# Twelve loads of a streaming encoder layer, issued by GpSimd instead of SyncE

## The chip, the cores and the metric

The kernel runs on one core of a Trainium2 chip. The metric is the device time of one execution in microseconds, the median of several runs. The five engines are named as the profile names them: PE (TensorE), DVE (VectorE), ACT (ScalarE), POOL (GpSimd) and SP (SyncE, which here only issues transfers). Each engine works through its own list of instructions in order; a transfer is issued by an instruction of an engine and then runs on the DMA engines by itself.

## What is computed

One layer of a streaming encoder for 384 rows: 256 prompt frames of one new stream and 16 frames of each of 8 running streams, all in float32.

```python
h = rmsnorm(x)                      # 384 x 2048
p = h @ w_in                        # columns: GLU in (2 x 1024) | q | k | v | forget logits | gates A, B
u = p[glu value] * sigmoid(p[glu gate])
A = conv branch: 31-tap causal depthwise conv over (old conv state, u), LayerNorm, swish, @ conv_pw_out
B = attention with a forget bias: running streams see 128 cached keys and values each; @ w_att_out
x = x + (sigmoid(gA) * A + sigmoid(gB) * B) @ w_out
x = x + (silu(conv3(g_half)) * u_half) @ w_down     # g_half, u_half = rmsnorm(x) @ w_up, d_ff 5632
```

Outputs are both groups' rows, the new keys, values and forget logits, and the new conv states.

## The kernel before

**Products.** Every large product streams its weights from HBM in tiles of 256 x 512 (`raw`, three buffers, issued by SP, `fetch`, L130). Each tile is split into `hi`, a rounded copy made by ACT (L139), and `lo`, the rest, made by DVE (L140); both have two buffers. PE then does three matmuls per block, hi by hi, lo by hi and hi by lo (L236 to L238), so PE needs each tile's `lo` soon after its `hi`. `gemm` walks through the tiles; after each 128 rows of weights it calls `tick`, which takes one step of each side job (generators). One such step of 9 matmuls is 2 us of PE at 512 columns.

**Side jobs in the first stages.** The stages are GLU (two pairs of a gate and a value product, 64 steps), V (48 steps), K and Q (32 each), then the gates. Beside them run:

- `weight_columns`: loads the old conv states, transposes them in 32 x 32 blocks on DVE (L250) and writes them through POOL to a DRAM tile `s_rows` (`quadrants_out`, four stores, L255). A load back from such a tile completes the transposition.
- `glu_pair`: when a pair is finished, `u` is evacuated, transposed the same way and written to `u_rows` by four POOL stores.
- `conv`: `load(n)` brings half of the old states (`sc`) and of the turned gated input (`uc`) back from `s_rows` and `u_rows`; `fill(c)` copies them on ACT into a tile `ext` (two buffers, L480 to L489; two small memsets by POOL, L482 and L483); `tap` does 31 multiply-adds on DVE (L496, L498) for each of eight tiles. The first `load` is emitted at step 37, the first `fill` at step 45, the second `load` with the 23rd tap of the third tile.
- `cached_keys`: from step 40 on, one head every 14 steps: the load `kc` of 128 keys of 8 streams (512 KB in rows of 512 bytes, L567), nine steps later the DVE transpose into `kw` (L250), then four POOL stores to a DRAM tile `keys`. `kc` and `kw` have one buffer each. The attention stage reads `keys` back by SP.

**What sets the order.** PE's order is the program's. For the other engines a planner in the tile framework lists the instructions ahead of time, by a priority that follows the order of the program (weight tiles and evacuations are raised by `high_priority`) and by its own idea of when each operand is ready; it may put an instruction far ahead of its place in the program. The list is then fixed, and the engine stops at an instruction whose operand is not there. `queued` adds one rule: a transfer is listed behind the newest transfer noted for its engine; with `False` as second argument it only becomes the newest. The transfers of later weight tiles are noted so, without being held. In the kernel before, all `queued` transfers but two go out on SP, and the stores of `quadrants_out` are not noted.

Of the kernel before, what the change touches and what calls it, by code (L numbers as in the profile page):

```python
# [40 lines left out]
def hybrid_step(  # L41
# [9 lines left out]
    nc = tc.nc  # L51
# [39 lines left out]
    def queued(d, chain=True):  # L91
        e = d.ins.engine
        if chain and e in newest:
            tc.add_manual_dep(d.ins, newest[e], mybir.DependencyInfo(
                mybir.DependencyClass.NoSync, mybir.DependencyReason.DATA), reason="queue")
        newest[e] = d.ins.name
# [152 lines left out]
    def swap_blocks(dst, src, q):  # L249
        nc.vector.transpose(dst.rearrange("p i q c -> p q i c"), src.rearrange("p (q i c) -> p q i c", q=q, i=4))  # L250

    def quadrants_out(src, n, d=None):
        d = d or p_dr.tile([4, 32, 4, n], F32, tag="turn", bufs=4, name="turn")
        for i in range(4):
            nc.gpsimd.dma_start(d[:, :, i, :].rearrange("j r n -> r j n"),  # L255
                                src[32 * i:32 * i + 32, :].rearrange("r (j n) -> r j n", j=4))
        return d

    def quadrants_in(dst, d, queue=None):
# [2 lines left out]
    def turned(rows, work, out):  # L262
        w = work.rearrange("p (i t q c) -> p i t q c", i=4, t=NTT, c=32)
        for t in range(NTT):
            swap_blocks(w[:, :, t], rows[:, t, :], 4)
        quadrants_in(out, quadrants_out(work, 384))
        return out.rearrange("p (i t q c) -> p i t q c", i=4, t=NTT, q=4)
# [173 lines left out]
    u_rows = [p_dr.tile([4, 32, 4, 384], F32, name=f"u_rows{i}") for i in range(2)]  # L441
    s_rows = p_dr.tile([4, 32, 4, 2, 256], F32, name="s_rows")

    def glu_pair(i):
        u = p_sg.tile([P, NTT, 512], F32, tag=f"S{2 + i}", name="u")
        cs = slice(512 * i, 512 * (i + 1))

        def gate(t, ps):
            nc.scalar.activation(u[:, t, :], ps[:], AF.Sigmoid, scale=rs1[:, t:t + 1])

        def value(t, ps):
            stt(u[:, t, :], ps[:], rs1[:, t:t + 1], u[:, t, :], op0=ALU.mult, op1=ALU.mult)

        def done():
            for t in range(NTT):
                swap_blocks(u_work[:, :, t], u[:, t, :], 4)
            quadrants_out(u_work[:].rearrange("p i t q c -> p (i t q c)"), 384, u_rows[i])
            nc.gpsimd.dma_start(sample_conv[0, :, 14:30, cs], u[:, 2, :])
            nc.gpsimd.dma_start(prompt_conv[0, 0, :, cs], u[98:128, 1, :])
        return job("B", 16, ha, gate), job("B", 16, ha, value, done=done)  # L460
# [3 lines left out]
    def conv():  # L464
        states, news, exts = {}, {}, {}

        def load(n):
            states[n] = p_cv.tile([P, 8, 4, 32], F32, tag="sc", bufs=1, name="sc")
            queued(nc.sync.dma_start(states[n][:].rearrange("p b q c -> p b (q c)"),
                                     s_rows[:, :, :, :, 128 * n:128 * (n + 1)].rearrange("j r i h n -> (j r) (i h) n")))  # L470
            news[n] = p_cv.tile([P, 4, NTT, 4, 32], F32, tag="uc", bufs=1, name="uc")
            queued(nc.sync.dma_start(news[n][:].rearrange("p i t q c -> p (i t q c)"),
                                     u_rows[n][:].rearrange("j r i n -> (j r) (i n)")))

        def fill(c):
            ext = exts[c] = p_cv.tile([P, 24, 46], F32, tag="ext", bufs=2, name="ext")
            e = ext[:].rearrange("p (i t h) x -> p i t h x", t=NTT, h=2)
            u = news[c // 4][:, :, :, c % 4, :].rearrange("p i t (h x) -> p i t h x", h=2)
            copy = nc.scalar.copy
            copy(e[:, :, 2, :, 0:30], states[c // 4][:, :, c % 4, 0:30].rearrange("p (i h) x -> p i h x", h=2))  # L480
            copy(ext[:, :, 30:46].rearrange("p (a h) x -> p a h x", h=2), u.rearrange("p i t h x -> p (i t) h x"))
            nc.gpsimd.memset(ext[:, 0, 0:30], 0.0)  # L482
            nc.gpsimd.memset(ext[:, 1, 0:14], 0.0)  # L483
            copy(e[:, :, 0:2, 1, 14:30], u[:, :, 0:2, 0, :])
            copy(e[:, 1:4, 0:2, 0, 14:30], u[:, 0:3, 0:2, 1, :])
            copy(e[:, 0, 1, 0, 14:30], u[:, 3, 0, 1, :])
            for h in range(2):
                copy(e[:, 1:4, 0:2, h, 0:14], u[:, 0:3, 0:2, h, 2:16])
            copy(e[:, 0, 1, :, 0:14], u[:, 3, 0, :, 2:16])  # L489

        def tap(c, w):
            v = exts[c][:, :, w:w + 16]
            o = ut[:, c, :].rearrange("p (a t) -> p a t", t=16)
            wc = cw[:, w * 8 + c:w * 8 + c + 1]
            if w == 0:
                ts(o, v, wc, col[:, R_DWB + c:R_DWB + c + 1], op0=ALU.mult, op1=ALU.add)  # L496
            else:
                stt(o, v, wc, o, op0=ALU.mult, op1=ALU.add)  # L498
            if w == CW - 1:
                if c == 1:  # L500
                    nc.gpsimd.tensor_tensor(sm[:], ut[:, 0, :], ut[:, 1, :], op=ALU.add)
                elif c > 1:
                    nc.gpsimd.tensor_tensor(sm[:], sm[:], ut[:, c, :], op=ALU.add)

        todo = [(c, w) for c in range(8) for w in range(CW)]
        done = due = 0
        for t in range(1 << 20):
            due += next(r for end, r in CONV_RATE if t < end)
            if t == CONV_START - 9:
                load(0)  # L510
            if t == CONV_START - 1:
                fill(0)
            while done < min(due, len(todo)):
                c, w = todo[done]
                tap(c, w)
                if w == 22 and c < 7:
                    fill(c + 1)
                    if c == 2:
                        load(1)
                done += 1  # L520
            if done == len(todo):
                return
            yield
# [38 lines left out]
    def cached_keys():  # L562
        for _ in range(KEYS_FIRST):
            yield
        for h in range(H):
            kc, work = (p_sg.tile([P, 8, P], F32, tag=f"S{i}", name=n) for i, n in enumerate(("kc", "kw")))
            queued(nc.sync.dma_start(kc[:], cache_k[0, :, :, h, :].rearrange("b p d -> p b d")))  # L567
            for _ in range(9):
                yield
            swap_blocks(work[:].rearrange("p b d -> p (b d)").rearrange("p (i b c) -> p i b c", i=4, b=8),  # L570
                        kc[:].rearrange("p b d -> p (b d)"), 8)
            key_rows[h] = p_dr.tile([4, 32, 4, 256], F32, name=f"keys{h}")
            quadrants_out(work[:].rearrange("p b d -> p (b d)"), 256, key_rows[h])
            for _ in range(KEYS_EVERY - 9):
                yield

    key_steps = cached_keys()

    gemm([glu_pair(i) for i in range(2)], [first_norm(), weight_columns(), conv_steps, key_steps])
# [4 lines left out]
    def tiny(name):  # L584
        return p_qkv.tile([P, NTT, H], F32, name=name)

    z, e, r, s2, pl = tiny("lz"), tiny("le"), tiny("lr"), tiny("ls"), tiny("lpoly")
# [531 lines left out]
```

## Time and profile before

| | us |
|---|---|
| median of 3 runs (lowest, highest) | 1997.26 (1996.68, 1998.42) |
| profiled execution | 1996.12 |
| its span, first to last instruction | 1994.4 |
| PE busy | 1982.1 |
| DVE, ACT, POOL busy | 1050.5, 774.4, 229.1 |

SP's transfer queue (q1) moved 275.16 MB, POOL's (q0) 67.69 MB. Times within the trace count from the start of the span. A timeline lists an engine's instructions by their start, with their duration; a bracket says how long the engine stood idle before one and which instruction or transfer ended that. The granted clock is TensorE's, as a share of full speed.

### The profile page before, as it was taken

To read this page: it belongs to the slowest core of one execution; us is meant where nothing else is said; L and a number is where in the kernel's file an instruction comes from. 1 tells how busy PE (TensorE), PEld (TensorE's weight loads), DVE (VectorE), ACT (ScalarE), POOL (GpSimd) and SP (SyncE) were. 2 spreads that over 40 slices of the span, in tenths; PEclk is the share of its full clock that TensorE was granted. 3 is DMA by queue.
4 is the path that set the end of the run, shared out by engine and by line. 5 is a ranking of instruction groups with operands and counts; after the bars stand their busy time and mean duration, and the time that the engine had idled before them with its cause. 6 is when DMAs were issued, how large, how long until landed. Compare 5 with 4: busy or idle time off the path is not lost.

```text
span 1994.4 us, 24094 instructions
## 1 busy us (share of the span) xinstructions
PE 1982.1 (99%) x9156; PEld 1645.2 (82%) x9156; DVE 1050.5 (53%) x1479; ACT 774.4 (39%) x1149; POOL 229.1 (11%) x492
## 2 busy tenths in 40 slices
PE   9999999999999999999999999999999999999999
PEld 7779888888888888888888888888888888888887
DVE  4489989643335447445454555343554554334543
ACT  4433353654324433445343444222433442223422
POOL 2002231100000002011211112000211120002100
PEclk9999999999999999999999999999999999999999
DMA  8556876654443448565656565444555554446553
GB/s 238 160 163 196 269 235 194 206 179 134 127 127 118 136 153 276 179 192 173 215 160 195 165 189 172 150 132 129 175 175 183 176 184 133 130 132 193 159 187 119
DMA packets 182563, 344.52 MB, mean 173 GB/s; under 512 B 15160, under 2 KB 47811, under 8 KB 182439
## 3 DMA queue, kind: packets, MB, share of 16 engines
q1 hardware_dynamic: 163711, 275.16, 45.1%
q0 software_dynamic: 18416, 67.69, 10.7%
q8 instruction: 71, 1.16, 0.2%
q14 instruction: 45, 0.37, 0.1%
q10 hardware_dynamic: 320, 0.14, 0.0%
HBM read 301.26 MB, written 42.14 MB: 172 GB/s over the span
## 4 chain that ended last, share of the span: by engine, by line
PE 90%; DVE 6%; issue 1%; DMA 1%; ACT 1%; POOL 0%; SPq 0%; DVEq 0%; POOLq 0%; ACTq 0%
PE acc L237 29%; PE acc L236 29%; PE acc L238 29%; DVE ut L498 3%; DVE lo L140 2%; PE misc L236 1%; PE misc L238 1%; PE misc L237 1%; DMA kc<-in_cache_k_dram 1%; DMA uc<-u_rows 0%; DVE qkw L250 0%; ACT hi L139 0%; PE misc L300 0%; PE misc L719 0%; PE misc L752 0%
## 5 line engine op out<-in xcount | busy, mean ns | idle before, releaser
L140 DVE TENSOR_TENSOR lo<-raw,hi 128x1024 fp32r<-128x1024 f32 (+2 forms) x481 | 579.5, 1205 | 828.3 <-ACT hi L139 822.3
L139 ACT CAST hi<-raw 128x1024 fp32r<-128x1024 f32 (+2 forms) x481 | 499.7, 1039 | 1062.0 <-PE acc L238 952.2
L237 PE MATMUL acc<-lo,xg 128*128 128x512 f32 x1056 | 410.9, 389 | 0.1
L238 PE MATMUL acc<-hi,xg 128*128 128x512 f32 x1056 | 410.8, 389 | 0.0
L236 PE MATMUL acc<-hi,xg 128*128 128x512 f32 x1056 | 410.8, 389 | 0.0
L237 PE MATMUL acc<-lo,hT 128*128 128x512 f32 (+1 forms) x880 | 334.1, 380 | 4.2 <-DVE lo L140 4.1
L236 PE MATMUL acc<-hi,hT 128*128 128x512 f32 (+1 forms) x880 | 337.9, 384 | 0.3 <-ACT hi L139 0.3
L238 PE MATMUL acc<-hi,hT 128*128 128x512 f32 (+1 forms) x880 | 333.8, 379 | 0.0
L237 PEld LDWEIGHTS acc<-lo,xg 128*128 128x128 f32 x1056 | 198.2, 188 | 41.6 <-DVE lo L140 0.5
L236 PEld LDWEIGHTS acc<-hi,xg 128*128 128x128 f32 x1056 | 198.2, 188 | 41.3
L238 PEld LDWEIGHTS acc<-hi,xg 128*128 128x128 f32 x1056 | 198.2, 188 | 41.1
L237 PEld LDWEIGHTS acc<-lo,hT 128*128 128x128 f32 x880 | 165.7, 188 | 36.3 <-DVE lo L140 8.9
L236 PEld LDWEIGHTS acc<-hi,hT 128*128 128x128 f32 x880 | 165.5, 188 | 30.4 <-issue 1.8
L238 PEld LDWEIGHTS acc<-hi,hT 128*128 128x128 f32 x880 | 165.4, 188 | 28.9
L236 PE MATMUL acc<-hi,act 128*128 128x512 f32 x484 | 188.3, 389 | 0.0
L237 PE MATMUL acc<-lo,act 128*128 128x512 f32 x484 | 188.3, 389 | 0.0
L238 PE MATMUL acc<-hi,act 128*128 128x512 f32 x484 | 188.3, 389 | 0.0
L255 POOL DMA_DIRECT2D turn<-block x124 | 68.1, 556 | 1031.5 <-DVE block L250 1004.9
L498 DVE SCALAR_TENSOR_TENSOR ut<-ext,cw,ut 128x384 f32<-128x384 f32 x240 | 138.4, 628 | 1.0
L238 PEld LDWEIGHTS acc<-hi,act 128*128 128x128 f32 x484 | 90.8, 188 | 19.0
L237 PEld LDWEIGHTS acc<-lo,act 128*128 128x128 f32 x484 | 90.8, 188 | 18.8
L236 PEld LDWEIGHTS acc<-hi,act 128*128 128x128 f32 x484 | 90.8, 188 | 18.7
(286 smaller groups left out, 1761.9 us busy)
## 6 DMA issues: line engine op xcount, KB each, us to landing
raw<-in_w_up_dram SPq DMA_DIRECT2D x176, 512.0 KB
raw<-in_w_in_dram SPq DMA_DIRECT2D x127, 512.0 KB
raw<-in_w_down_dram SPq DMA_DIRECT2D x88, 512.0 KB
turn<-block POOLq DMA_DIRECT2D x120, 192.0 KB, 4.1
block<-turn POOLq DMA_DIRECT2D x30, 768.0 KB, 6.0
raw<-in_w_out_dram SPq DMA_DIRECT2D x32, 512.0 KB
raw<-in_w_in_dram SPq DMA_DIRECT2D x24, 344.0 KB
raw<-in_w_att_out_dram SPq DMA_DIRECT2D x16, 512.0 KB
```

The source lines that it names most:

```text
L139: nc.scalar.copy(hi[:, k, :o], raw[:, k, :o])
L140: tt(lo[:, k, :o], raw[:, k, :o], f(hi[:, k, :o]), op=ALU.subtract)
L236: mm(o, ah[:, s], hi[:, kk, :n], start=st, stop=False)
L237: mm(o, ah[:, s], lo[:, kk, :n], start=False, stop=False)
L238: mm(o, al[:, s], hi[:, kk, :n], start=False, stop=sp)
L255: nc.gpsimd.dma_start(d[:, :, i, :].rearrange("j r n -> r j n"), src[32 * i:32 * i + 32, :].rearrange("r (j n) -> r j n", j=4))
L498: stt(o, v, wc, o, op0=ALU.mult, op1=ALU.add)
```

## The change

The eight loads of `kc`, the two of `sc` and the two of `uc` are issued by POOL instead of SP. The four stores of `quadrants_out`, on POOL before and after, are now noted as POOL's newest transfer, so that each of these loads is listed behind the POOL store or load emitted last before it. Nothing else is altered; the loads of `keys` by SP stay.

```diff
     def quadrants_out(src, n, d=None):
         d = d or p_dr.tile([4, 32, 4, n], F32, tag="turn", bufs=4, name="turn")
         for i in range(4):
-            nc.gpsimd.dma_start(d[:, :, i, :].rearrange("j r n -> r j n"),
-                                src[32 * i:32 * i + 32, :].rearrange("r (j n) -> r j n", j=4))
+            queued(nc.gpsimd.dma_start(d[:, :, i, :].rearrange("j r n -> r j n"),
+                                       src[32 * i:32 * i + 32, :].rearrange("r (j n) -> r j n", j=4)), False)
         return d
...
             states[n] = p_cv.tile([P, 8, 4, 32], F32, tag="sc", bufs=1, name="sc")
-            queued(nc.sync.dma_start(states[n][:].rearrange("p b q c -> p b (q c)"),
+            queued(nc.gpsimd.dma_start(states[n][:].rearrange("p b q c -> p b (q c)"),
...
             news[n] = p_cv.tile([P, 4, NTT, 4, 32], F32, tag="uc", bufs=1, name="uc")
-            queued(nc.sync.dma_start(news[n][:].rearrange("p i t q c -> p (i t q c)"),
+            queued(nc.gpsimd.dma_start(news[n][:].rearrange("p i t q c -> p (i t q c)"),
...
-            queued(nc.sync.dma_start(kc[:], cache_k[0, :, :, h, :].rearrange("b p d -> p b d")))
+            queued(nc.gpsimd.dma_start(kc[:], cache_k[0, :, :, h, :].rearrange("b p d -> p b d")))
```

## Rows read from the trace of the kernel before

**Rows 1.** The page, part 1: busy us, share of the span, instructions of each engine.

```profile
PE 1982.1 (99%) x9156; PEld 1645.2 (82%) x9156; DVE 1050.5 (53%) x1479; ACT 774.4 (39%) x1149; POOL 229.1 (11%) x492
```

**Rows 2.** Stretches, PE alone: from and to, us, busy, granted clock, DMA share, GB/s.

```profile
0.00:25.00 25.00, 21.81 (x108) 1.00 0.82 247
...
1975.00:2000.00 25.00, 14.86 (x66) 0.91 0.09 32
```

**Rows 3.** Timeline of PE: matmuls that waited, 80 to 140; start, us, instruction.

```profile
81.45 0.50 PE L237 MATMUL acc<-lo,hT 128*128 128x512 f32 x1 [0.25 <-DVE lo L140]
99.28 0.50 PE L237 MATMUL acc<-lo,hT 128*128 128x512 f32 x1 [1.23 <-DVE lo L140]
113.65 0.50 PE L237 MATMUL acc<-lo,hT 128*128 128x512 f32 x1 [1.69 <-DVE lo L140]
```

**Rows 4.** Stretches of 2 us: PE, PEld, DVE, ACT, POOL busy, granted clock, DMA.

```profile
112.00:114.00 2.00, 0.35 (x2) 0.31 (x3) 2.00 (x3) 0.72 (x1) 0.00 (x0) 1.00 0.00 0
114.00:116.00 2.00, 2.00 (x8) 1.57 (x7) 2.00 (x5) 0.00 (x0) 0.00 (x0) 0.67 0.60 146
116.00:118.00 2.00, 2.00 (x6) 1.58 (x5) 2.00 (x4) 0.00 (x0) 0.00 (x0) 0.50 0.30 116
118.00:120.00 2.00, 2.00 (x10) 1.59 (x9) 2.00 (x5) 0.55 (x1) 0.00 (x0) 0.97 0.76 197
```

**Rows 5.** Timeline of DVE, 90 to 113.

```profile
90.80 1.22 DVE L140 TENSOR_TENSOR lo<-raw,hi 128x1024 fp32r<-128x1024 f32 x1 [2.85 <-ACT hi L139]
96.88 1.25 DVE L250 STREAM_TRANSPOSE kw<-kc 128x1024 f32<-128x1024 f32 x1 [4.85 <-DMA kc<-in_cache_k_dram]
...
109.22 0.48 DVE L496 TENSOR_SCALAR ut<-ext,cw,col 128x384 f32<-128x384 f32 x1 [3.39 <-ACT ext L489]
...
112.37 1.22 DVE L140 TENSOR_TENSOR lo<-raw,hi 128x1024 fp32r<-128x1024 f32 x1
```

**Rows 6.** The chain that ended last: start, us from issue to landing.

```profile
88.38 8.47 DMA kc<-in_cache_k_dram
...
99.79 7.85 DMA uc<-u_rows
```

**Rows 7.** Timeline of ACT, 107 to 111.

```profile
107.67 0.52 ACT L481 COPY ext<-uc 128x384 f32<-128x384 f32 x1 [3.10 <-DMA uc<-u_rows]
...
110.36 1.05 ACT L139 CAST hi<-raw 128x1024 fp32r<-128x1024 f32 x1
```

**Rows 8.** Timeline of SP: its issues (xcount: that many within the time).

```profile
88.38 1.48 SPq L567 DMA_DIRECT2D kc<-in_cache_k_dram  x1
92.05 7.57 SPq L130 DMA_DIRECT2D raw<-in_w_in_dram  x2
...
268.17 0.46 SPq L567 DMA_DIRECT2D kc<-in_cache_k_dram  x1
```

**Rows 9.** Timeline of POOL, first stages and feed-forward part.

```profile
10.89 0.12 POOL L482 MEMSET ext<- 128x30 f32 x1
...
86.61 2.18 POOL L255 DMA_DIRECT2D u_rows<-u_work  x4 [1.16 <-DVE u_work L250]
98.42 2.18 POOL L255 DMA_DIRECT2D keys<-kw  x4 [9.62 <-DVE kw L250]
...
983.33 2.19 POOL L255 DMA_DIRECT2D turn<-block  x4 [5.19 <-DVE block L250]
991.54 0.56 POOL L260 DMA_DIRECT2D block<-turn  x1 [6.02 <-DMA turn<-block]
```

**Rows 10.** Line 260, POOL's loads of turned tiles.

```profile
DMA to landing us min/median/max: 4.5/5.8/7.2
```

**Rows 11.** Waits: engine, line, waited for; us in total, times, longest us.

```profile
DVE kw L250 <- DMA kc<-in_cache_k_dram: 6.7, 3, 4.9
...
ACT block L953 <- DMA block<-turn: 2.0, 4, 0.6
...
ACT extf L1000 <- DMA block<-turn: 0.8, 1, 0.8
```

More of the change, by code (lines that the diff above doesn't have):

```diff
@@ L468, in load @@
             states[n] = p_cv.tile([P, 8, 4, 32], F32, tag="sc", bufs=1, name="sc")
-            queued(nc.sync.dma_start(states[n][:].rearrange("p b q c -> p b (q c)"),
-                                     s_rows[:, :, :, :, 128 * n:128 * (n + 1)].rearrange("j r i h n -> (j r) (i h) n")))
+            queued(nc.gpsimd.dma_start(states[n][:].rearrange("p b q c -> p b (q c)"),
+                                       s_rows[:, :, :, :, 128 * n:128 * (n + 1)].rearrange("j r i h n -> (j r) (i h) n")))
             news[n] = p_cv.tile([P, 4, NTT, 4, 32], F32, tag="uc", bufs=1, name="uc")
-            queued(nc.sync.dma_start(news[n][:].rearrange("p i t q c -> p (i t q c)"),
-                                     u_rows[n][:].rearrange("j r i n -> (j r) (i n)")))
+            queued(nc.gpsimd.dma_start(news[n][:].rearrange("p i t q c -> p (i t q c)"),
+                                       u_rows[n][:].rearrange("j r i n -> (j r) (i n)")))
         def fill(c):
```

## The prediction

> **What bounds the kernel now.** I read the page's busy table first, then PE's busy time in stretches of 25 us, then every place where a matmul waited, and only there the other engines. The reader is to see that TensorE is the bound nearly everywhere: it is busy for 1982.1 us [rows 1] of a span of 1994.4, so only 12.3 us are idle in all. Of these, the first 25 us hold 25.00 - 21.81 = 3.19 and the tail after 1975 holds 19.4 - 14.86 = 4.54 [rows 2], and neither is near the change. The other 4.57 us lie in between, most of them in two places, both in the second half of the GLU stage: 1.23 us ahead of the matmul at 99.28 and 1.69 us ahead of the one at 113.65 [rows 3]. Both end when VectorE delivers a split weight (lo). A third wait, 0.25 us at 81.45, comes from VectorE's own evacuation work there, and I leave it as it is.
>
> The second wait has a consequence that idle time does not show. Right behind it the granted clock is 0.67, 0.50 and 0.97 in three stretches of 2 us [rows 4], before and after it 1.00: the engine runs partly at 1.2 instead of 2.4 GHz, and loses 2 x (0.33 + 0.50 + 0.03) = 1.72 us. The shorter wait at 98 has no such fall behind it. So what can be won here is 1.23 + 1.69 + 1.72 = 4.64 us, 0.23% of the time; even if every idle moment between start and tail went too, it would be 4.57 + 1.72 = 6.3 us.
>
> **Why these two waits are there.** At 96.88 VectorE turns the first cached-key tile (kw from kc). It works in order, so it stood still for 4.85 us until kc had landed [rows 5]; SP had issued kc at 88.38, 8.47 us earlier [rows 6]. The lo behind it came late, and PE waited 1.23 us. Then ScalarE waited 3.10 us for uc, the turned gated input, which was issued at 99.79 and took 7.85 us [rows 6]. The twelve copies of two conv tiles ran from 107.67 to 110.36, where the next weight's hi starts [rows 7]; VectorE first waited 3.39 us for them and then worked on conv taps from 109.22 to 112.37, ahead of the lo that PE needed [rows 5]. Both loads landed later than the order on an in-order engine had room for.
>
> **The change part by part.**
>
> *SP gives up twelve issues* (eight kc, two sc, two uc). One occupies SP for 0.46 to 1.48 us [rows 8]. But SP is not short of time: the lo at 90.80 ends at 92.02 [rows 5], and the weight that waits for its buffer is issued at 92.05 [rows 8]. Gain: 0. The cover is the three weight buffers; without it, one long issue of 1.48 us would stand in a weight's way.
>
> *POOL takes twelve issues.* The four stores of a turned block take 2.18 us [rows 9], so one issue is 0.55 and twelve are 6.5 us, on an engine that is busy 11% of the span [rows 1]. Price on the path: 0. The bytes stay the same, 8 x 0.52 + 2 x 0.52 + 2 x 0.79 = 6.8 MB, which leave SP's queue for POOL's.
>
> *The new order.* Each store now counts as the newest transfer of POOL, and each load is put behind the newest. In program order these are the stores of u_rows, then sc, uc, then kc of head 0, so on POOL this order is forced: the u_rows stores are issued from 86.61 to 88.79 [rows 9], sc right behind, and uc must wait until the stores have landed. How long that is, the same pair shows later: stores issued until 985.52, the load at 991.54, 6.0 us behind [rows 9]. uc is then issued at 94.8 and kc at 95.4. Meanwhile POOL holds up nothing that is wanted: its next work now is at 98.42 [rows 9], and that itself follows from kc. A load of this pattern lands in 4.5 to 7.2 us [rows 10]; the two that SP issued here took 7.85 and 8.47. So uc lands at 99.3 to 102.6 instead of 107.64, and kc at 99.9 to 103.9 instead of 96.85: uc 5 to 8 us earlier, kc of head 0 3 to 7 us later.
>
> *The other heads.* Before, a kc stood behind the weight traced just ahead of it, and the last went out at 268.17 [rows 8]. Behind its preceding store it has no weight to follow, and the planner moves work forward where it can (a memset of the conv stage, emitted behind 45 steps of the product loop, ran at 10.89 [rows 9]). One round of 6 us landing, 1.25 transposing [rows 5], 2.2 storing and, as I guess, 2.5 until VectorE is free makes 12 us: head 1's kc goes at about 106 and the last at 106 + 6 x 12 = 178, some 90 us earlier than now. The second uc, no longer behind a weight either, goes at about 170 to 180. The transposes keep their price, 8 x 1.25 us on VectorE. Of the seven I count no idle PE: before, three of eight kc were waited for, 6.7 us in all [rows 11], and only the first cost PE time. Bounds: 0, and 7 x 1.23 = 8.6 us if each did what the first did. I take 0, as for the other two of the three.
>
> *What goes and what is late next.* The order on ScalarE and VectorE is worked out anew, so the places change. What counts is whether a load lands later than its consumer's place in that order. The consumers of POOL's loads in the later stages had to wait five times, 2.8 us in all and never over 0.8 [rows 11], although a store and a load stand in a row there; those of the SP loads here waited 4.85 and 3.10. So I expect the first wait (1.23), the second (1.69) and its clock loss (1.72) to go. Next in line are the same kw and the same twelve copies at new places, close together, after a stretch full of transfers. For this I put back one wait without a fall of the clock, the nearest row being the 1.23 us at 99.28 [rows 3]; its bounds are 0 and 1.69 + 1.72 = 3.41.
>
> Sum: 4.64 - 1.23 = 3.41 us less. The profiled execution took 1996.12 us (the span and 1.7 around it), which gives 1992.7; the median of the three runs is 1.14 above it, so **1993.9 us**.
>
> The Trainium skill, "DMA: Bandwidth & Descriptors", section "Issuing engines are not separate DMA queues", speaks against any gain: transfers started by any engine run on the same 16 DMA engines, and another issuing engine only saves the time of the issue. By that rule the sum would be 0, since SP's issue time is hidden; the trace agrees on the issue time, but the place in an in-order queue moves too, and that the rule does not weigh. The same page's "Specifications" give about 1 us to the first byte on GpSimd's path and 0.6 on SP's; by them each load would come 0.4 us later (an estimate from that page), while the rows show POOL's loads of 768 KB landing no later than SP's.
>
> **The rivals.**
>
> *All of it goes.* POOL's loads land where the order has them and nothing is put back: 4.64 us less, 1997.26 - 4.64 = 1992.6. For it: the short waits behind POOL's loads. Against: here two loads, the stores and the weights come at once, which the later stages do not have.
>
> *The waits only move.* uc lands earlier, but its consumers are placed earlier as well; ScalarE waits some 3 us for it again, with 1.69 us of idle PE and the slow clock behind it, and only kw's wait is gone: 1.23 us less, 1996.0; with kw's wait back too, 1997.3. For it: the same two kinds of work on the same in-order engines. Against: uc then stands on the kind of load that was waited for least. It is the case that the skill's sentence above leads to.
>
> *kw waits longer: slower.* If kw of head 0 keeps its place behind the lo of 90.80, VectorE stands until kc lands, now up to 7.0 us later (103.9). The place is VectorE from 92 to 104, the price 1.23 + 7.0 = 8.2 us of idle PE and one fall of the clock of 1.72, less the 4.64 of now: +5.3 us, 2002.6. It decides for slower when kc lands behind 102.6 with kw still there (1.23 + 5.8 + 1.72 - 4.64 = +4.1). For it: uc and then kc stand behind a wait for a landing, which is new. Against: there are about 3 us of free VectorE between two lo [rows 5], in which a kw that is planned later fits.
>
> **How the numbers follow.** Forecast (one small wait left, 1992.8 to 1995.3): 0.35. All goes: 0.25. Waits only move (1995.3 to 1998): 0.25. Slower: 0.15. About 0.2%, 4.0 us, is what a measurement can tell from no change; faster then means below 1993.3: the case in which all goes and a small part of the forecast's, 0.28. Slower means above 2001.3: most of its case, 0.13. The rest, 0.59, lies within. The range from 1991.6 to 2000.5 leaves out the upper part of the slow case and the chance that more idle time than these two waits goes.
>
> **What would show it.** POOL's queue gains 6.8 MB; uc is issued at about 95 and kc of head 0 right behind; the last kc goes before 200. PE has no wait of over a microsecond between 96 and 100 or between 110 and 116, and a granted clock of 1.00 there; VectorE's waits for kc are below 4.85 each. The forecast is wrong if PE's idle time between 75 and 200 does not fall below 2 us, if a new wait of over 1.7 us stands anywhere, or if the clock falls at another place.

## The result: 0.2% slower, by a wait that the forecast did not look at

The changed kernel takes 2000.99 us (median of 14 runs, 1999.94 to 2004.58), the kernel before 1997.10 in the runs beside it. The ratio is 1.0022, interval 1.0013 to 1.0030: 3.9 us slower, where 3.4 us faster was forecast. The profiled execution has a span of 1998.4 us, 4.0 more than before.

The page of the changed kernel, busy time and the two transfer queues: PE is busy for 2 us more, POOL for 9, and 6.8 MB have gone from SP's queue (q1) to POOL's (q0), as reckoned.

```profile
PE 1984.1 (99%) x9156; PEld 1647.0 (82%) x9156; DVE 1053.4 (53%) x1479; ACT 773.7 (39%) x1149; POOL 238.2 (12%) x504
...
q1 hardware_dynamic: 153023, 268.34, 44.0%
q0 software_dynamic: 20144, 74.51, 12.0%
```

First the order that the change forces on POOL. The timeline of POOL in the changed kernel:

```profile
87.52 2.18 POOL L255 DMA_DIRECT2D u_rows<-u_work  x4 [1.16 <-DVE u_work L250]
89.69 0.92 POOL L469 DMA_DIRECT2D sc<-s_rows  x1
95.43 0.57 POOL L472 DMA_DIRECT2D uc<-u_rows  x1 [4.82 <-DMA raw<-in_w_in_dram]
96.93 0.91 POOL L567 DMA_DIRECT2D kc<-in_cache_k_dram  x1 [0.93 <-issue]
...
176.91 0.90 POOL L567 DMA_DIRECT2D kc<-in_cache_k_dram  x1
177.80 0.89 POOL L469 DMA_DIRECT2D sc<-s_rows  x1
178.68 0.56 POOL L472 DMA_DIRECT2D uc<-u_rows  x1
...
206.09 0.92 POOL L567 DMA_DIRECT2D kc<-in_cache_k_dram  x1
```

It is the order worked out ahead: sc, uc and kc right behind the stores of u_rows, uc at 95.43 (94.8 was said), the last kc at 206 instead of 268 [rows 8], the second uc at 178.68 instead of 218.02. The trace names a weight's transfer as the one that ended the wait ahead of uc; what uc waits for by the program is the landing of u_rows, and the traces of e6 and e7 name that.

PE in the stretch of the two old waits [rows 3], in pieces of 25 us (busy, granted clock, DMA share, GB/s):

```profile
75.00:100.00 25.00, 24.75 (x110) 1.00 0.67 202
100.00:125.00 25.00, 25.00 (x112) 1.00 0.76 218
```

Both waits and the fall of the clock are gone. VectorE waits for no kc at all any more. But these are the matmuls of the changed kernel that waited, from 80 to 300 (two of 0.27 and 0.17 left out):

```profile
82.36 0.50 PE L237 MATMUL acc<-lo,hT 128*128 128x512 f32 x1 [0.25 <-DVE lo L140]
...
188.76 0.42 PE L236 MATMUL acc<-hi,hT 128*128 128x344 f32 x1 [1.01 <-ACT hi L139]
189.68 0.42 PE L237 MATMUL acc<-lo,hT 128*128 128x344 f32 x1 [0.49 <-DVE lo L140]
...
237.49 1.01 PE L619 MATMUL misc<-uo,lg 128*8 128x256 f32 x2 [3.55 <-DVE lg L602]
...
289.07 0.50 PE L237 MATMUL acc<-lo,hT 128*128 128x512 f32 x1 [0.57 <-DVE lo L140]
```

And the stretches of 2 us around 237, PE alone:

```profile
236.00:238.00 2.00, 0.51 (x2) 0.85 0.71 205
238.00:240.00 2.00, 2.00 (x9) 0.50 0.26 64
240.00:242.00 2.00, 2.00 (x7) 0.80 0.09 23
```

The great new wait stands ahead of L619, the first of the small products that turn the forget logits `lg` into bias rows: 3.55 us, and a fall of the clock of 2 x (0.15 + 0.50 + 0.20) = 1.70 us behind it. The reader is to look at what ended it: not a weight, but L602 of VectorE, the last of a chain of 16 tiny dependent operations on VectorE, with one of ScalarE among them (L588 to L602). VectorE in the changed kernel, first the first tap of the fifth conv tile, then the end of this chain:

```profile
213.35 0.48 DVE L496 TENSOR_SCALAR ut<-ext,cw,col 128x384 f32<-128x384 f32 x1
...
231.06 0.17 DVE L599 SCALAR_TENSOR_TENSOR lpoly<-lpoly,ls 128x24 f32<-128x24 f32 x1
231.15 0.61 DVE L498 SCALAR_TENSOR_TENSOR ut<-ext,cw,ut 128x384 f32<-128x384 f32 x1
231.68 0.17 DVE L599 SCALAR_TENSOR_TENSOR lpoly<-lpoly,ls 128x24 f32<-128x24 f32 x1
231.77 0.60 DVE L498 SCALAR_TENSOR_TENSOR ut<-ext,cw,ut 128x384 f32<-128x384 f32 x1
...
237.18 0.17 DVE L602 SCALAR_TENSOR_TENSOR lg<-lpoly,lz 128x24 f32<-128x24 f32 x1
```

Each link takes 0.17 us, but a conv tap of 0.6 stands behind nearly each: taps of the fifth and sixth tile, the first that read the second uc. The fifth tile's taps begin at 213.35; in the kernel before they begin at 227.98, when the chain is half done. So the 39 us by which the second uc goes out earlier have become 15 us for its taps. The chain begins at 222.11 and ends at 237.35: 15.2 us. In the kernel before it went from 223.07 to 232.69, 9.6 us, and PE came to L619 at 235.06, with 2.4 us to spare. The first link, the fifth tile's first tap, the last link and PE's first bias product there:

```profile
223.07 0.18 DVE L588 TENSOR_TENSOR lz<-vt,bf 128x24 f32<-128x24 f32 x1
...
227.98 0.47 DVE L496 TENSOR_SCALAR ut<-ext,cw,col 128x384 f32<-128x384 f32 x1
...
232.51 0.18 DVE L602 SCALAR_TENSOR_TENSOR lg<-lpoly,lz 128x24 f32<-128x24 f32 x1
...
235.06 0.60 PE L619 MATMUL misc<-uo,lg 128*8 128x256 f32 x2
```

The other new wait, 1.50 us at 188, comes from a weight that was late. ScalarE there:

```profile
187.95 1.43 ACT L139 CAST hi<-raw 128x688 fp32r<-128x688 f32 x2 [5.06 <-DMA raw<-in_w_in_dram]
```

It is the stretch behind 176.91, where a kc, sc and uc go out within 2 us.

The sum of what the two traces show: 4.64 us gone, 1.50 + 3.55 + 1.70 + 0.57 = 7.3 come, a few tenths each way. That is 2.7 us. A further 0.9 us lies ahead of 82 us, where the matmul of 81.45 [rows 3] now starts at 82.36; in the profiles below the same matmul starts between 81.40 and 82.57 with no relation to the edit, so I don't count it as an effect. Of the remaining 1.2 of the 3.9 us, about 0.4 lies outside the span: the 14 times of the changed kernel are 2.1 to 2.2 us longer than their spans, the profiled execution of the kernel before only 1.7. The other 0.8 I can't place.

### The profile page after: what moved, and what is told of

The parts are those of the page before. It is cut to its first block, busy times and chain, and to the rows that moved or that the text cites. A ratio compares the mean times of both kernels' runs of the same rounds, so it can differ in the third digit from the quotient of the medians.

```text
span 1998.4 us, 24098 instructions
## 1 busy us (share of the span) xinstructions
PE 1984.1 (99%) x9156; PEld 1647.0 (82%) x9156; DVE 1053.4 (53%) x1479; ACT 773.7 (39%) x1149; POOL 238.2 (12%) x504
## 4 chain that ended last, share of the span: by engine, by line
PE 89%; DVE 8%; issue 1%; DMA 1%; ACT 0%; POOL 0%; SPq 0%; DVEq 0%; POOLq 0%; ACTq 0%
PE acc L237 28%; PE acc L236 28%; PE acc L238 28%; DVE ut L498 4%; DVE lo L140 3%; PE misc L238 1%; PE misc L236 1%; PE misc L237 1%; DMA raw<-in_w_in_dram 0%; PE misc L300 0%; ACT hi L139 0%; DVE kw L250 0%; PE misc L752 0%; PE misc L719 0%; DMA bs<-c_dr 0%
## 5 line engine op out<-in xcount | busy, mean ns | idle before, releaser
L498 DVE SCALAR_TENSOR_TENSOR ut<-ext,cw,ut 128x384 f32<-128x384 f32 x240 | 143.7, 632 | 2.0
```

## The experiments

Theory A: the cost comes from one of the twelve loads' moves, the second uc (with its sc), which is there 39 us earlier; conv taps of the next tiles are then at hand while the `lg` chain runs, and PE, in order, waits for it. The rivals put it to the eight kc, to the POOL path as such, or to VectorE being too full. The kernel before took 1997.36 beside the first four and 1997.19 beside the other four.

### e1: the second pair by SP

```diff
-            queued(nc.gpsimd.dma_start(states[n][:]...
+            queued((nc.sync if n else nc.gpsimd).dma_start(states[n][:]...
-            queued(nc.gpsimd.dma_start(news[n][:]...
+            queued((nc.sync if n else nc.gpsimd).dma_start(news[n][:]...
```

> The changed kernel, but the second sc and uc are issued by SP again; the first pair and all kc stay on POOL. Theory A (the second uc comes 39 us earlier, so conv taps fill VectorE between the links of the forget-logit chain, L588 to L602, and the bias product of PE, L619, waits): the wait ahead of L619 falls from 3.55 us to below 0.3, the fall of the clock behind it (1.7 us) goes, and with the burst of sc, uc and kc at 177 to 188 the wait of 1.5 us at 188 goes too: 2001.0 - 5.2 - 1.5 = 1994.3 us, 0.14% below the kernel before. Rival B (the eight kc in quick succession fill VectorE and the queues): L619 still waits over 2.5 us, 2000 to 2001.5. Rival C (the POOL path as such costs time at many places): no single wait changes by over 1 us, 1999 to 2001.

Measured: 1993.17 us (1991.31 to 1994.18), ratio to before 0.9979, 0.9970 to 0.9987. uc goes out at 215.25. Between 85 and 600 two matmuls wait, and the granted clock is 1.00 in every stretch of 25 us:

```profile
208.06 0.42 PE L237 MATMUL acc<-lo,hT 128*128 128x344 f32 x1 [0.25 <-DVE lo L140]
217.41 0.51 PE L237 MATMUL acc<-lo,hT 128*128 128x512 f32 x1 [0.44 <-DVE lo L140]
```

The chain runs from 220.07 to 231.54, 11.5 us. The ten loads that stay on POOL thus earn 4.2 us against the kernel before, near the 4.64 at stake, and the two others cost 3.9 + 4.2 = 8.1 us, each kernel taken against the kernel before in the runs beside it (the two medians alone are 7.8 apart). B and C fall, since the eight kc and ten of the POOL issues are still there. This version beats both kernels.

### e2: only the keys on POOL

```diff
-            queued(nc.gpsimd.dma_start(states[n][:]...
+            queued(nc.sync.dma_start(states[n][:]...
-            queued(nc.gpsimd.dma_start(news[n][:]...
+            queued(nc.sync.dma_start(news[n][:]...
```

> Only the eight kc on POOL; both sc and both uc by SP as before. Theory A: no long wait ahead of L619 (below 0.5 us); the two old waits at 99 and 113 stay in some form (uc's by all means, 1.69 and 1.72 of clock), so 1995.5 to 1998, the same as before. Rival B: L619 waits over 2.5 us and the time is 1999 to 2002.

Measured: 1998.13 us, ratio 1.0005, 0.9996 to 1.0014: no difference from before. L619 does not wait, so the kc are cleared again. But my account of the rest missed. Both old waits are gone although uc is issued by SP: at 96.65, where the kernel before has 99.79 [rows 6]. The chain that ended last in the kernel before, between its two rows of [rows 6], shows why:

```profile
98.04 1.20 DVE lo L140
...
99.26 0.37 SPq L130
```

The lo that stood behind kw freed the buffer of the weight that SP issued at 99.26, and uc stood behind that weight. So the second old wait followed in part from the first. In e2 the kw comes two lo later in VectorE's order (at 100.07), this weight goes out at 96.10 and uc right behind it. In place of the old waits, small ones for lo are spread over V, K and Q, nine of over 0.2 us with 4.8 us in all, of which these are the largest:

```profile
170.82 0.43 PE L237 MATMUL acc<-lo,hT 128*128 128x344 f32 x1 [1.02 <-DVE lo L140]
...
334.60 0.50 PE L237 MATMUL acc<-lo,hT 128*128 128x512 f32 x1 [0.93 <-DVE lo L140]
```

SP issued the second uc only at 228.72 here. That the later taps are what makes the lo late is likely, but was not tried.

### e3: only sc and uc on POOL

```diff
-            queued(nc.gpsimd.dma_start(kc[:]...
+            queued(nc.sync.dma_start(kc[:]...
```

> Only sc and uc on POOL; the eight kc by SP as before. The second pair then stands behind a store of keys, which comes at its old time of about 198 to 200, so uc is there some 15 us earlier than in the kernel before, not 39. Theory A: conv taps are again at hand when the forget-logit chain runs (222 to 236), L619 waits 2 to 4 us with a fall of the clock, the old wait at 113 is gone: 1997.1 - 3.4 + 5.2 = 1998.9, at least 1998. Rival B: the L619 wait is below 0.5 and 1993.7 to 1995 comes out.

Measured: 2002.77 us, ratio 1.0026, 1.0016 to 1.0037. The second uc goes out at 202.33.

```profile
101.07 0.50 PE L237 MATMUL acc<-lo,hT 128*128 128x512 f32 x1 [2.57 <-DVE lo L140]
...
240.13 1.01 PE L619 MATMUL misc<-uo,lg 128*8 128x256 f32 x2 [3.33 <-DVE lg L602]
```

L619 waits as theory A has it, without a single kc moved. The time is 4 us above the expectation: the wait for kw, whose kc SP issued at its old place, grew from 1.23 to 2.57 us and has a fall of the clock behind it (0.58 and 0.57 in the next two stretches of 2 us), 1.11 us of waiting for a lo at 178 are new, and the clock behind L619 is low for longer than in the changed kernel (0.50, 0.50 and 0.58 from 240 to 246).

### e4: the bias products four steps later

```diff
     def bias_rows():
-        for _ in range(6):
+        for _ in range(10):
```

> The changed kernel with one number altered: the bias products of PE (L619 to L627) come 10 steps behind the V stage instead of 6, some 8 us later; all twelve loads stay on POOL. Theory A: what costs is only that PE stands in order behind the late chain; the wait ahead of L619 and the clock fall go, 2001.0 - 5.2 = 1995.8 us, and the 1.5 us at 188 stay. Rival B (VectorE has too much to do there, whoever waits): as much idle time, over 3 us, appears ahead of weights between 230 and 260, and the time stays above 1999.

Measured: 1996.08 us, 4.9 less than the changed kernel; ratio to before 0.9996, 0.9987 to 1.0005. The chain is as late as ever, but PE comes later still:

```profile
236.18 0.18 DVE L602 SCALAR_TENSOR_TENSOR lg<-lpoly,lz 128x24 f32<-128x24 f32 x1
```

```profile
187.78 0.42 PE L236 MATMUL acc<-hi,hT 128*128 128x344 f32 x1 [0.68 <-ACT hi L139]
188.69 0.43 PE L237 MATMUL acc<-lo,hT 128*128 128x344 f32 x1 [0.49 <-DVE lo L140]
...
266.24 0.50 PE L237 MATMUL acc<-lo,hT 128*128 128x512 f32 x1 [0.87 <-DVE lo L140]
```

L619 starts at 241.05 without a wait, and no fall of the clock is left. What cost the time was PE's place in the order, not VectorE's load; only 1.8 us of small waits come back between 260 and 290.

### e5: the second pair alone, in the kernel before

```diff
-            queued(nc.sync.dma_start(states[n][:]...
+            queued((nc.gpsimd if n else nc.sync).dma_start(states[n][:]...
-            queued(nc.sync.dma_start(news[n][:]...
+            queued((nc.gpsimd if n else nc.sync).dma_start(news[n][:]...
```

> The kernel before with the second sc and uc alone moved to POOL; the first pair and all kc stay on SP, and the stores are not noted. Theory A (a second uc that is there before the forget-logit chain makes PE wait at L619): the pair goes out as soon as the copies of the fourth conv tile are done, at about 170 to 200; L619 waits 2.5 to 4 us with a fall of the clock of about 1.7 behind it, and the two old waits at 99 and 113 stay: 1997.3 + 5 = 2002.3, at least 2000. Rival C (moving loads to POOL costs by their number, a little each): two of twelve loads cost at most 1 us, 1997 to 1998.5.

Measured: 2006.15 us (5 runs), ratio 1.0049, 1.0037 to 1.0062. uc goes out at 170.17.

```profile
100.83 0.50 PE L237 MATMUL acc<-lo,hT 128*128 128x512 f32 x1 [1.65 <-DVE lo L140]
115.36 0.50 PE L237 MATMUL acc<-lo,hT 128*128 128x512 f32 x1 [1.69 <-DVE lo L140]
...
244.65 1.01 PE L619 MATMUL misc<-uo,lg 128*8 128x256 f32 x2 [2.97 <-DVE lg L602]
```

Two loads of the twelve are enough for all of the loss and more. It is larger than expected: six further waits of half a microsecond to 1.1 us appear between 170 and 306, and the granted clock behind L619 is 0.50 from 244 to 250, where the changed kernel has 0.50 for 2 us only.

### e6: e1 and e4 together

```diff
+            queued((nc.sync if n else nc.gpsimd).dma_start(...
-        for _ in range(6):
+        for _ in range(10):
```

> The second pair by SP and the bias products 10 steps behind V instead of 6, together. Theory A: both changes take away the same wait, so the second adds nothing: 1993.2 us as with the first alone, within 0.8 us. Rival B (moving the bias products eases VectorE by itself): another 3 to 5 us less, 1988 to 1990.

Measured: 1993.10 us, ratio 0.9980, 0.9971 to 0.9989: the same as e1. Where nobody waits for the chain, moving its reader is worth nothing.

### e7: the second pair on POOL, behind the last kc

```diff
+                if (c, w) == (3, 21):
+                    load(1)
                 tap(c, w)
...
                     fill(c + 1)
-                    if c == 2:
-                        load(1)
```

> All twelve loads on POOL as in the changed kernel, but the second sc and uc are emitted one conv tile later, so that they stand behind the last kc, at about 207 instead of 178. uc then lands at about 214, still ahead of the forget-logit chain (222). Theory A: the transfers at 177 to 188 are no longer bunched, so the 1.5 us at 188 go, but the wait ahead of L619 stays at 2 us or more with its fall of the clock: 1998.5 to 2000. Rival D (what counts is how early uc comes: 39 us are too much, 10 are not): L619 waits below 0.5 us, 1993.5 to 1995.

Measured: 2001.02 us, ratio 1.0022, 1.0013 to 1.0031; uc goes out at 204.64.

```profile
226.74 0.50 PE L237 MATMUL acc<-lo,hT 128*128 128x512 f32 x1 [1.10 <-DVE lo L140]
236.55 0.59 PE L619 MATMUL misc<-uo,lg 128*8 128x256 f32 x2 [3.59 <-DVE lg L602]
```

The wait at 188 is gone, so it did come from the three loads in a bunch; but 0.76 us at 217 and 1.10 at 226 come, which puts the time a microsecond above the expectation. The wait ahead of L619 is undiminished, though uc comes 26 us later than in the changed kernel: what decides is whether its taps are there when the chain runs (here the fifth tile's begin at 218.04, the chain at 219.75), not by how much uc is early. Rival D falls.

### e8: the second pair on POOL, behind the last stores

```diff
-                if w == 22 and c < 7:
+                if w == (30 if c == 3 else 22) and c < 7:
+                    if c == 3:
+                        load(1)
                     fill(c + 1)
-                    if c == 2:
-                        load(1)
```

> All twelve loads on POOL, but the second sc and uc and the copies of the fifth conv tile are emitted with the last tap of the fourth tile, behind the stores of the last keys: issued at about 218 to 224, as late as SP issued them before. Theory A: taps of the fifth tile are not at hand during the chain, L619 waits below 0.5 us without a fall of the clock, the bunch at 177 is gone: 1993 to 1995, as with the second pair on SP. Rival C (the POOL path itself costs the time): 1999 or more.

Measured: 1998.50 us, ratio 1.0007, 0.9998 to 1.0016. Half right. No tap is at hand during the chain, which runs from 220.36 to 226.36 in 6.0 us; L619 does not wait. But sc, issued at 221.27, lands 8.3 us later, and ScalarE stands at its copy with the next weight's hi behind it:

```profile
229.62 0.69 ACT L480 COPY ext<-sc 128x240 f32<-128x240 f32 x2 [6.64 <-DMA sc<-s_rows]
```

```profile
231.31 0.50 PE L236 MATMUL acc<-hi,hT 128*128 128x512 f32 x1 [1.30 <-ACT hi L139]
232.57 0.50 PE L237 MATMUL acc<-lo,hT 128*128 128x512 f32 x1 [0.76 <-DVE lo L140]
```

Behind these the granted clock is 0.91, 0.50 and 0.73 for 2 us each. It is the old kind of wait at a new place. Its 1.30 + 0.76 us and the 2 x (0.09 + 0.50 + 0.27) = 1.72 of the clock, 3.8 us in all, are about the distance from the expected 1993 to 1995. Whether SP's path would have brought sc sooner at that moment was not tried, so against rival C this run says only that its mark, 1999, was not reached.

### The chain over all profiles

| kernel | second uc issued | first tap of the fifth tile | chain, us | wait ahead of L619, us |
|---|---|---|---|---|
| before | 218.02 | 227.98 | 9.6 | none |
| changed | 178.68 | 213.35 | 15.2 | 3.55 |
| e1 | 215.25 | 226.17 | 11.5 | none |
| e2 | 228.72 | 236.10 | 8.2 | none |
| e3 | 202.33 | 214.44 | 14.5 | 3.33 |
| e4 | 178.01 | 212.37 | 15.2 | none (reader moved) |
| e5 | 170.17 | 211.49 | 15.9 | 2.97 |
| e6 | 214.30 | 225.62 | 11.9 | none (reader moved) |
| e7 | 204.64 | 218.04 | 16.6 | 3.59 |
| e8 | 222.18 | 233.79 | 6.0 | none |

Wherever uc goes out by 205, the fifth tile's taps begin before the chain does (at 219.75 to 228.60), the chain takes over 14 us and L619 waits, unless it is moved away; from 214 on, none of this.

## Why the prediction was wrong, step by step

- **What bounds the kernel, and the two waits:** right in the bound and in the stake: the 4.64 us went, and in e1, where little new takes their place, 4.2 us are won. But the two waits were counted as two late loads, each with a wait of its own, and in the kernel before the first load held up the second; e2, which moves no uc, clears both.
- **SP's and POOL's issues at no price:** right in effect. A kc takes POOL 0.90 us, not 0.55, but in the changed kernel no wait of PE, VectorE or ScalarE between 80 and 300 ended with work of POOL.
- **The new order on POOL:** right, to within 1.6 us for uc and kc. The trace gives 5.0, 6.7 and 8.5 us (least, median, most) for the landing of kc, longer than the 4.5 to 7.2 of [rows 10], and VectorE still never waited for one.
- **The other heads:** the kc went earlier, but not as early as said (last kc at 206, said 178), mainly by one gap of 28.6 us between two of them; the price of the transposes was nothing, as said, to judge by e1, which has all eight. This part has the step that failed: "The second uc, no longer behind a weight either, goes at about 170 to 180." The time was right; that an operand which comes 39 us earlier costs nothing was taken for granted. I gave it no price and no bound. By e1 it is worth 8.1 us; in e5, moved alone, 9.
- **What goes and what is late next:** wrong. I looked for the next late thing among the loads' own consumers (kw and the twelve copies). The next late thing was a chain that touches none of the moved data, and had 2.4 us to spare ahead of PE: the trace of before showed L602 at 232.51 and L619 at 235.06, and I did not look there. The 1.23 us put back stand against 7.3 that came.
- **The rivals:** the slow one had a late kw as its mechanism; no kw waited. The right side, with the wrong cause. The wait at 188 belongs to none of them either.
- **The marks of being wrong:** they served. A wait of 3.55 us stands where 1.7 was the limit, the clock falls at another place (238), and PE's idle time between 75 and 200 is 2.02 us, just not below 2.
- **The rule of the Trainium skill** ("DMA: Bandwidth & Descriptors", "Issuing engines are not separate DMA queues") that another issuing engine only saves issue time leaves out the place in an in-order list, as the forecast said: by it nothing would change, while the new places of ten loads earned 4.2 us (e1) and those of the other two cost 8.1.

## What to carry to other kernels

An operand that comes earlier is not free when a planner fills the gaps of a busy in-order engine (VectorE, in the changed kernel: 192 of the 200 us from 100 to 300): its consumers become ready work and slip between the links of any chain of short dependent operations there. Before you call an earlier load harmless, list the chains on that engine in the time gained, and how much each has to spare ahead of the engine that sets the end. When one edit moves several loads, try each alone: here ten of twelve earned 4.2 us and two cost 8.1. And before two late loads are counted as two waits, see whether the first holds up the issue of the second.

## What the runs showed of the hardware that I had not expected

The granted clock does not follow the length of one wait. 1.69 us of idle PE at 112 in the kernel before were followed by 1.72 us of loss [rows 4]; the same 1.69 us in e5 were followed by stretches at 1.00 throughout:

```profile
114.00:116.00 2.00, 0.64 (x3) 1.00 0.00 0
116.00:118.00 2.00, 2.00 (x11) 1.00 0.70 196
118.00:120.00 2.00, 2.00 (x10) 1.00 0.18 67
```

Behind each of the longer waits after the first 80 us, 2.57 to 3.59 us (changed kernel, e3, e5, e7), it fell. What the wait of 1.69 us costs can thus be its own length or twice that, and no run here tells which beforehand.
